# Three small matmuls on constants behind each half-tile unit of the last stages

## The chip, the cores and the metric

One core of a Trainium2 chip. The metric is device time in microseconds (us) of one execution; a smaller time is better. Each kernel was run several times, and one run of each left a trace. Two times appear: the execution's time, and the span, from the first to the last instruction of the trace. The comparisons ran on three chips (numbered 2, 3 and 4 in the results), each with the kernel before in the same rounds, so a ratio is a sounder figure than a difference of times from two sections.

## The reference

`x` is 8 x 2048 x 2048 in fp32, `bias` is 8 x 256. Each row of 2048 is 8 heads of 256. The result is a log-sum-exp per head, each value written twice.

```python
x_heads = x.reshape(B, S, H, Dh).transpose(0, 2, 1, 3)
x_heads = x_heads + bias[None, :, None, :]
x_tiled = np.repeat(x_heads, 2, axis=2)
mx = x_tiled.max(axis=-1, keepdims=True)
lse = mx.squeeze(-1) + np.log(np.exp(x_tiled - mx).sum(axis=-1))
```

The kernel reads 134 MB and computes little per byte. It takes the exponential without subtracting the maximum.

## The kernel before

64 tiles of 256 rows (2 MB) pass through nine SBUF buffers. In tiles 0 to 56 a tile is one unit. In tiles 57 to 63, the last stages, a tile is two units of 1 MB, one per row of a partition (`k`); below, (58,0) is the first unit of tile 58. The units are small so that less is left to do when the last byte lands.

```python
STAGES = [
    (0, (BULK,)),                      # g0=4: GpSimd adds the bias of heads 4 to 7
    (54, (MIXED,)),                    # g0=4
    (57, (PROMPT_F1, PROMPT_F1)),      # g0=8: GpSimd adds no bias
    (62, (SINGLE_F1, SINGLE_F1)),
    (63, (PROMPT_F2, TRIPLE)),
]
```

In tiles 57 to 63 the first one to three heads of a unit go by TensorE: one matmul puts the bias (3 bf16 parts, 3 rows) into a PSUM bank, a second adds `x` through an identity, and ScalarE takes the exponential with a sum. The other heads are exponentiated in place by ScalarE, and multiplied by exp(bias) and summed by VectorE, one or two of them (none in the last unit) by GpSimd.

```python
            if m["late"]:
                pe_part = late_heads(m, t, bias_here, sums)
            else:
                heads = add_x(m, t, k0, c0, c1, bias_here)   # x matmuls, wait for the load
                ...
            if c0 == 0:
                if next_units and not m["late"]:
                    bias_there = put_bias(*next_units.pop(0))  # bias matmul of the next unit
                if m["g0"] < H:
                    add = g_add(m, t, k0, k1)
                if t < T - 1 or k0 == 0:
                    flush(for_pool)
            ...
            if c0 == 0:
                flush(for_pe)      # ScalarE: heads of the unit before
```

A batch's sums are transposed by TensorE into one half of the bank `tpair`, and ScalarE takes the logarithm from there. Batch 6's transposes stand at the end of tile 57 and use `tps[0]`; those of the last batch use `tps[1]`.

The softmax here doesn't subtract the row's maximum and nothing guards it: scores larger than these inputs give would overflow.

## Time and profile before

| | before |
|---|---|
| time, median of 3 | 327.21 us (327.03 to 327.37) |
| span of the profiled run | 326.0 us (it took 327.84 us, more than these three) |
| HBM traffic over the span | 415 GB/s |
| TensorE busy | 263.2 us, 81% |
| mean granted TensorE clock | 0.877 |

Three views carry the argument, and the prediction shows their lines: the page's row PEclk (TensorE clock that was granted, in tenths, in 40 slices), the chain that ended last, and TensorE's instructions in order of time. An fp32 matmul appears as two matmul records (two passes), so a line with x2 is one matmul of the program.

### The profile page before, as it was taken

The page shows a single profiled execution, that of the slowest core. Times are in us where ns is not written, and L with a number is a line of the kernel's source. Part 1 is how long each engine was busy: PE and PEld are TensorE (multiplying, and loading weights), DVE is VectorE, ACT ScalarE, POOL GpSimd, SP SyncE. Part 2 cuts the span into 40 slices and gives each one's busy share as a digit, 9 for nine tenths or more (in the row PEclk, how much of TensorE's full clock was granted, in tenths as well). Part 3 has the DMA queues.
Part 4 walks back from the last instruction along what each step waited for, and adds up shares of the span by engine and source line. Part 5 has one row for each costly group of instructions (what it writes and reads, how often), then busy time and mean ns, then how long its engine had stood idle before and what let it go on. Part 6 is the DMA issues. An engine that isn't in the chain of part 4 may idle for free.

```text
span 326.0 us, 2182 instructions
## 1 busy us (share of the span) xinstructions
PE 263.2 (81%) x565; PEld 90.5 (28%) x565; DVE 283.8 (87%) x306; ACT 263.6 (81%) x425; POOL 290.5 (89%) x123
## 2 busy tenths in 40 slices
PE   4488999599987998878878688688879887498885
PEld 1123333133332333223323223223323222121221
DVE  1005999999999999999989998979998989999994
ACT  1119999489994999698689869879887797999995
POOL 6999999899999999999999999999999899858873
PEclk9999999779995999799799979978997797657755
DMA  8999999999999999999999999999999999999994
GB/s 297 433 428 428 432 424 427 432 420 432 432 422 432 432 417 434 430 420 431 431 422 430 431 422 426 434 422 428 434 424 427 430 426 422 418 423 421 421 387 126
DMA packets 11933, 135.41 MB, mean 415 GB/s; under 512 B 1361, under 2 KB 1745, under 8 KB 2961
## 3 DMA queue, kind: packets, MB, share of 16 engines
q1 hardware_dynamic: 11824, 135.27, 98.7%
q8 instruction: 4, 0.07, 0.1%
q14 instruction: 7, 0.06, 0.0%
q10 hardware_dynamic: 2, 0.01, 0.0%
q0 software_dynamic: 96, 0.00, 0.0%
HBM read 134.23 MB, written 1.05 MB: 415 GB/s over the span
## 4 chain that ended last, share of the span: by engine, by line
DVE 41%; DMA 39%; PE 7%; ACT 6%; POOL 5%; issue 1%; SPq 0%
DVE R L342 36%; DMA xt<-in_x_dram 36%; DVE xt L335 6%; ACT xt L323 4%; PE pair L267 3%; POOL xt L317 3%; DMA b<-bparts 2%; PE one_ps L267 2%; PE pair L249 2%; ACT xt L285 1%; DMA brow<-in_bias_dram 1%; ACT xt L298 1%; POOL brest L173 1%; POOL brest L171 1%; PE pair L231 0%
## 5 line engine op out<-in xcount | busy, mean ns | idle before, releaser
L317 POOL TENSOR_TENSOR xt<-xt,b_rep 128x2048 f32<-128x2048 f32 x57 | 258.7, 4542 | 19.6 <-DMA xt<-in_x_dram 19.6
L342 DVE TENSOR_REDUCE R<-xt 128x14 f32<-128x3584 f32 (+1 forms) x56 | 214.5, 3830 | 1.9
L323 ACT ACTIVATE xt<-xt 128x2560 f32<-128x2560 f32 (+5 forms) x77 | 158.5, 2068 | 10.9 <-POOL xt L317 10.6
L267 PE MATMUL pair<-xt,ident 128*128 128x512 f32 x216 | 116.3, 666 | 0.0
L267 PE MATMUL one_ps<-xt,ident 128*128 128x512 f32 x108 | 65.8, 694 | 21.2 <-DMA xt<-in_x_dram 21.2
L285 ACT ACTIVATE xt<-pair 128x1024 f32<-128x1024 f32 x54 | 56.7, 1050 | 19.9 <-PE pair L267 18.5
L267 PEld LDWEIGHTS pair<-xt,ident 128*128 128x128 f32 x216 | 46.2, 214 | 60.9 <-issue 60.9
L335 DVE TENSOR_TENSOR xt<-xt,w_ps 128x512 f32<-128x512 f32 x54 | 36.7, 681 | 28.0 <-ACT xt L323 27.9
L278 ACT ACTIVATE xt<-one_ps 128x256 f32<-128x256 f32 x108 | 41.1, 400 | 8.1 <-PE one_ps L267 8.0
L249 PE MATMUL pair<-xt,ident 128*128 128x512 f32 (+1 forms) x36 | 30.3, 946 | 7.8 <-DMA xt<-in_x_dram 7.6
L214 PE MATMUL one_ps<-b,ones 3*128 3x512 bf16 x54 | 20.8, 386 | 18.2 <-ACT xt L278 12.1
L214 PEld LDWEIGHTS <-ones 3*128 3x128 bf16 x162 | 13.6, 92 | 71.6 <-issue 65.5
L214 PE MATMUL pair<-b,ones 3*128 3x512 bf16 x108 | 32.3, 378 | 0.0
L267 PEld LDWEIGHTS one_ps<-xt,ident 128*128 128x128 f32 x108 | 17.0, 198 | 44.0 <-DMA xt<-in_x_dram 35.1
L278 ACT ACTIVATION_READ_ACCUMULATOR xt<-one_ps 128x1 f32 x108 | 24.5, 227 | 0.0
L358 DVE CUSTOM_DVE_ANT_0 xt<-xt,w_ps 128x256 f32<-128x256 f32 x61 | 22.4, 418 | 0.0
L382 POOL TENSOR_TENSOR xt<-xt 128x128 f32<-128x128 f32 (+3 forms) x39 | 13.9, 356 | 3.1
L374 POOL TENSOR_TENSOR xt<-xt,w_sb 128x256 f32<-128x256 f32 (+1 forms) x13 | 10.0, 773 | 5.2 <-ACT xt L323 4.5
L298 ACT ACTIVATE xt<-pair 128x256 f32<-128x256 f32 x33 | 12.4, 389 | 0.6 <-PE pair L249 0.6
L249 PEld LDWEIGHTS pair<-xt,ident 128*128 128x128 f32 x36 | 8.2, 278 | 16.7 <-DMA xt<-in_x_dram 13.1
L413 ACT ACTIVATE res<-tpair 64x512 f32<-64x512 f32 x7 | 4.1, 590 | 8.7 <-PE tpair L403 8.5
L358 DVE CUSTOM_DVE_ANT_0 xt<-xt,one_ps 128x256 f32<-128x256 f32 x27 | 10.6, 415 | 0.5 <-ACT xt L323 0.5
(38 smaller groups left out, 60.6 us busy)
## 6 DMA issues: line engine op xcount, KB each, us to landing
xt<-in_x_dram SPq DMA_DIRECT2D x57, 2048.0 KB, 29.1
xt<-in_x_dram SPq DMA_DIRECT2D x12, 1024.0 KB, 24.7
xt<-in_x_dram SPq DMA_DIRECT2D x4, 256.0 KB, 11.4
out_dram<-res SPq DMA_DIRECT2D x1, 896.0 KB, 6.7
xt<-in_x_dram SPq DMA_DIRECT2D x2, 384.0 KB, 15.8
xt<-in_x_dram SPq DMA_DIRECT2D x2, 128.0 KB, 6.3
out_dram<-res_last SPq DMA_DIRECT2D x1, 128.0 KB, 1.7
b<-bparts POOLq DMA_DIRECT2D x3, 1.5 KB, 6.5
```

Of the source, the lines that this page charges most:

```text
L214: nc.tensor.matmul(p, lhsT=ones3, rhs=each_row(b3, h * Dh, Dh, K), start=True, stop=False,)
L249: mm = nc.tensor.matmul(p, lhsT=ident, rhs=xts[t % NBUF][:, ka:kb, c : c + w], start=False, stop=True,)
L267: mm = nc.tensor.matmul(p, lhsT=ident, rhs=xts[t % NBUF][:, :, h * Dh : (h + 1) * Dh], start=False, stop=True,)
L278: act = nc.scalar.activation(out=xts[t % NBUF][:, k, 0:Dh], in_=got[0][:, k * Dh : (k + 1) * Dh], func=ACT.Exp, accum_out=sums[:, k, 0:1],)
L285: act = nc.scalar.activation(out=xts[t % NBUF][:, :, Dh : m["pe"] * Dh].rearrange("p k (h j) -> p h k j", j=Dh), in_=got[-1].rearrange("p ...
L298: act = nc.scalar.activation(out=xts[t % NBUF][:, k, h * Dh : (h + 1) * Dh], in_=p, func=ACT.Exp, accum_out=sums[:, k, h : h + 1],)
L317: add = nc.gpsimd.tensor_tensor(out=v, in0=v, in1=each_row(b_rep, c - G0, D - c, k1 - k0), op=ALU.add)
L323: return on_x(t, nc.scalar.activation(out=v, in_=v, func=ACT.Exp), [after])
L335: mul = nc.vector.tensor_tensor(out=f, in0=f, in1=each_row(w_ps, m["pe"] * Dh - W0, n, k1 - k0), op=ALU.mult,)
L342: red = nc.vector.tensor_reduce(out=sums[:, k0:k1, h0:H], in_=v.rearrange("p k (h j) -> p k h j", j=Dh), op=ALU.add, axis=mybir.AxisListTy ...
L358: ttr = nc.vector.tensor_tensor_reduce(out=v, in0=v, in1=w, scale=1.0, scalar=0.0, op0=ALU.mult, op1=ALU.add, accum_out=dst,)
L382: done = nc.gpsimd.tensor_tensor(out=v[:, :, 0:n], in0=v[:, :, 0:n], in1=v[:, :, n : 2 * n], op=ALU.add)
```

## The change

The intent is to keep TensorE's clock from being halved in the last stages: TensorE is given work that nobody needs, so that it looks busy. The output goes to the half bank `tps[0]`, which nothing reads after batch 6's logarithm.

```diff
+NWARM = 3
...
+    def keep_warm():
+        for _ in range(NWARM):
+            nc.tensor.matmul(
+                tps[B % 2][:, 0], lhsT=ident, rhs=ident, start=True, stop=True
+            )
...
                 if next_units and not m["late"]:
                     bias_there = put_bias(*next_units.pop(0))
+                if t > T_PROMPT and m["g0"] == H:
+                    keep_warm()
                 if m["g0"] < H:
                     add = g_add(m, t, k0, k1)
```

`T_PROMPT` is 54, so this holds for tiles 57 to 63: 14 units, 42 matmuls.

## The prediction

> **What bounds the kernel now.** I read the page first. Its slices show the 16 DMA engines full up to the last slice but one, and a granted TensorE clock that falls at the end:
>
> ```profile
> PEclk9999999779995999799799979978997797657755
> DMA  8999999999999999999999999999999999999994
> ```
>
> The next view is the chain that ended last, asked for the last 75 us, by line and then in order of time:
>
> ```profile
> by line: DMA xt<-in_x_dram 75.6%; PE pair L249 7.5%; ACT xt L323 6.7%; POOL xt L317 6.5%; ACT xt L298 2.9%; PE pair L231 1.8%; PE tpair L424 0.7%; ACT res_last L430 0.5%; issue 0.3%
> ...
> 294.61 19.87 DMA xt<-in_x_dram
> 314.48 0.04 issue
> 314.52 1.22 PE pair L249 x2
> 315.75 0.53 PE pair L231
> 316.28 2.01 PE pair L249 x2
> 318.29 0.75 PE pair L231 x2
> 319.04 2.02 PE pair L249 x2
> 321.06 0.02 issue
> 321.08 0.84 ACT xt L298 x4
> ```
>
> Loads set the end until 314.5 us. From there the chain is TensorE alone, for 6.5 us: the last units' x matmuls (L249) and bias matmuls (L231). Then come the last heads' exponentials, a transpose, a logarithm and the store. So TensorE time added late is on the chain; TensorE time added earlier is hidden if TensorE keeps up with the loads. Whether it does is seen in the timeline of TensorE, at the start of the changed stretch and at two later places:
>
> ```profile
> 287.20 2.08 PE L249 MATMUL pair<-xt,ident 128*128 128x512 f32 x2
> 289.21 0.60 PE L231 MATMUL pair<-b,ones 3*128 3x512 bf16 x1
> 289.74 2.08 PE L249 MATMUL pair<-xt,ident 128*128 128x512 f32 x2
> 291.75 0.60 PE L231 MATMUL pair<-b,ones 3*128 3x512 bf16 x1
> ...
> 304.54 1.12 PE L249 MATMUL pair<-xt,ident 128*128 128x512 f32 x2
> 305.60 0.39 PE L231 MATMUL pair<-b,ones 3*128 3x512 bf16 x1
> ...
> 312.01 1.22 PE L249 MATMUL pair<-xt,ident 128*128 128x256 f32 x2
> 313.16 0.39 PE L231 MATMUL pair<-b,ones 3*128 3x256 bf16 x1
> ```
>
> A unit at 289 us starts 2.54 us after the one before (287.20 to 289.74). A unit is half a tile, 1 MB, and the page's 420 GB/s or so brings one each 2.5 us. So TensorE at this clock is just saturated. At 304.5 us the same x matmul takes 1.06 us start to start instead of 2.01. The stage table in slices of 2 us gives the reason, the granted clock (third column from the right):
>
> ```profile
> 294.00:296.00 2.00, 1.98 (x5) 0.48 (x4) 2.00 (x8) 2.00 (x6) 1.76 (x5) 1.00 1.03 430
> 296.00:298.00 2.00, 0.95 (x2) 0.45 (x2) 2.00 (x14) 2.00 (x6) 1.77 (x5) 0.79 1.00 418
> 300.00:302.00 2.00, 2.00 (x3) 0.16 (x2) 2.00 (x13) 2.00 (x6) 1.74 (x4) 0.50 1.01 414
> ```
>
> In slices of 0.25 us it is 0.50 from 280.1, 1.00 from 293.8, 0.50 from 297.2, 1.00 from 304.0, and 0.50 from 307.4 to the end. TensorE runs the whole last stretch at half clock, while the change's name (keep warm) says what it is for.
>
> **What the Trainium skill says.** "TensorE: Matmul & The Clock Gate", Part 1, has a clock that is half or full and is set by a free-running activity window of about 3.4 us. This trace agrees: its late switches lie 3.4 us or multiples of it apart (256.2, 259.6, 269.9, 273.3, 280.1). The promise "full after one busy window" agrees only in part: TensorE was occupied from 284.66 to 293.75, 9.1 us, before the clock rose. The same page, "Back-to-back issue gap", has small matmuls with their weight loads at about 81 ns for N=128 against 56 ns alone, so some 45% on top of streaming; no such run of small non-transposing matmuls is in this trace. "PSUM — Partial Sum Buffer", "PSUM bank collisions raise a hardware error", asks for waits by bank between engines. The trace doesn't show whether the new writes will wait, but the program order below decides it.
>
> **The change, part by part.** Nothing is removed. Tiles 57 to 63 (g0 is 8) have two units each, so 14 units gain 3 fp32 matmuls of 128x128 on the identity, 42 in all. They stand behind the unit's x matmul and the next unit's bias matmul, so ahead of the next unit's x matmul.
>
> Cost of one. An fp32 matmul is two passes (x2). In a stream of 512 columns passes start 0.43 us apart at full clock and 0.85 at half (weight loads at 265.51 and 265.94, at 319.98 and 320.83). A quarter of the columns streams 0.107 or 0.213 us per pass. The weight load in such a stream is recorded as 0.19 and 0.33 us, longer than that, so it will not hide completely. I take streaming plus a quarter, an estimate between the page's 45% and full hiding: 0.14 and 0.27 us. Six passes: 0.85 us at full clock, 1.6 at half.
>
> A unit on TensorE, from the timeline above:
> - half clock: 2.01 + 0.53 + 1.6 = 4.1 us per 2.5 us of loads; it falls behind by 1.6 us per unit;
> - full clock: 1.06 + 0.36 + 0.85 = 2.3 us; it regains 0.2 us per unit, busy 92% of the time. Windows that kept the full clock were busy as little as 67 to 75% (263.0 to 266.5 had 2.55 of 3.50 us; 273.3 to 276.7 had 2.29 of 3.40), those that lost it 53 to 63%. So once full, it should stay full.
>
> The start. Unit (57,0) begins at 287.20 at half clock, because the stage before left TensorE idle. Two units then cost about 4.1 and 2.5 to 4.1 us until the clock rises at about 293.8, as before. Unit (58,0) starts at about 295.3 instead of 292.7: 2.6 us late. At 0.2 us per unit 1.4 us of this is regained by tile 62, whose units are shorter (0.65 + 0.3 + 0.85 = 1.8 us), which regains 0.7 us each. So (63,0) starts about 0.5 us late, at some 316.8. On the chain from there: x 1.06, two bias 0.5, three small 0.85, then x of (63,1) in two parts, 1.06 and 0.55, with three small between, 0.85. Sum 4.9 us, so TensorE ends at 321.7, against 321.9 before. The warm clock pays for the added work and no more.
>
> What the last heads need besides. ScalarE works without a gap from 314.5 to 320.5, and waits for TensorE only 0.57 us (321.08 minus its last wide exponential's end). Even a free TensorE could not gain more than that: 0.6 us, 0.2%.
>
> The new wait. The logarithm of batch 6 reads the bank that unit (58,0)'s small matmuls write, so TensorE waits there for ScalarE. The transposes before that logarithm also move, from 292.3 to about 295; ScalarE reaches the logarithm at 294.53, so it stops for some 0.8 us. ScalarE is 2.5 us behind the loads then and takes 2.1 us per unit against their 2.5, so it regains this by about tile 62; there 0.4 us may be left and cancels most of the gain.
>
> Heads read one unit later than TensorE makes them (at 302.64 the heads of (59,0), made by 299.03: 3.6 us of room), so 2.6 us of delay stops ScalarE little. The last load was issued at 314.5 behind a queue of loads and frees no buffer that these units hold, so loads do not move.
>
> Sum for this course: 0.0 us, within about 0.5 either way.
>
> **Rivals.**
> 1. The small matmuls cost more. If a pass takes as long as the recorded weight load, 0.19 us at full clock, six take 1.14 and a unit 2.56 us: the early delay is never regained. TensorE ends near 325, 3 to 3.5 us late: 330.5 us. For it: a load of 0.19 against streaming of 0.107. Against it: that record also holds fixed latency (the first load of a burst takes 0.15).
> 2. The clock rises one window later, at 297.2. Then one more unit runs at 4.1 us, and the end is about 2 us late: 329.3. For it: two saturated windows from 297.2 were needed before the rise at 304.0. Against it: the added matmuls fill all 128 rows, as those of the bulk stage do, where one busy window was enough (269.9 to 273.3).
> 3. The clock never rises, or falls again at the end. Fourteen units at 4.1 us from 287.2 end past 340: 345 us, 5% slower. Against it: a TensorE with a backlog is busy all the time, and was always granted the full clock in the end.
> 4. A clear gain: TensorE at full clock ends well before ScalarE. Bounded by the 0.57 us wait: 326.6 us.
>
> **Range and chances.** The central course gives 327.2; rival 1 (about 1 in 4, +3.3 us) and rival 2 (about 1 in 4, +2 us) can add, rival 3 has about 1 in 20. I name 328.2, and a range of 326.7 to 333. Faster by over 2% would need 6.5 us; only 0.57 us waits there: 0.01. Slower by over 2% needs over 6.5 us: rival 3, or 1 and 2 together: 0.09. Within 2%: 0.90.
>
> **What would show it.** The changed profile should show 42 more fp32 matmuls (84 more records); PEclk near 10 in the last seven slices instead of 657755; 0.8 to 0.9 us from the first small matmul to the next work; x of (58,0) near 295; loads landing as before; and the chain's end either TensorE or ScalarE within 0.5 us of each other. Small passes at 0.19 us or more would prove rival 1; a clock still 0.50 after 297 rival 2. I would be wrong altogether if the clock stayed low with TensorE full, or if a delayed ScalarE pushed the loads.
>
> The predicted time is 328.2 us.

## The result and the profile after

| | before | after |
|---|---|---|
| time, median of 4 runs each | 327.29 us (327.03 to 327.61) | 326.81 us (326.80 to 327.16) |
| time, second comparison | 327.49 us (11 runs) | 326.61 us (326.55 to 326.70, 5 runs) |
| span of the profiled run | 326.0 us | 325.4 us |
| mean granted clock | 0.877 | 0.921 |
| TensorE busy, records | 263.2 us, 565 | 263.2 us, 649 |

Ratios are the mean time of one kernel's fast runs over the mean of the other's of the same rounds, so not quite the ratio of the medians. The first comparison gave 0.9988 with a 95% interval of 0.997 to 1.0005, which includes no change. The second, with more runs, gave 0.9975 (0.9963 to 0.9987): the change gains 0.25%, some 0.8 us. It is inside 2%, so "the same" by this study's measure, and also real.

The page of the changed kernel, its granted clock and the DMA engines' share in 40 slices:

```profile
PEclk9999999899979987997997979798998989569999
DMA  7999999999999999999999999999999999999995
```

The last four slices read 9999 where they were 7755. In slices of 0.25 us the clock rises to 1.00 at 290.8 us and stays there past the last computation. The loads are as full as before. The 84 new records are there, yet TensorE's busy time in this trace did not grow by a tenth of a microsecond: its x matmuls (L251) took 21.0 us in all instead of 30.3, so the higher clock paid for them.

TensorE's instructions of the changed kernel in order of time (start, duration, line, output and inputs; L251 adds x, L233 puts the bias, L266 is the new line):

```profile
289.60 1.50 PE L266 MATMUL tpair<-ident 128*128 128x128 f32 x6
290.94 1.02 PE L251 MATMUL pair<-xt,ident 128*128 128x512 f32 x2
...
295.04 0.94 PE L266 MATMUL tpair<-ident 128*128 128x128 f32 x6 [0.49 <-ACT res L421]
...
297.08 0.94 PE L266 MATMUL tpair<-ident 128*128 128x128 f32 x6
297.85 1.02 PE L251 MATMUL pair<-xt,ident 128*128 128x512 f32 x2
298.81 0.39 PE L233 MATMUL pair<-b,ones 3*128 3x512 bf16 x1
299.12 0.94 PE L266 MATMUL tpair<-ident 128*128 128x128 f32 x6
```

The cost from start to start: three small matmuls take 0.77 us at full clock (297.08 to 297.85) and 1.34 us at half (289.60 to 290.94), so 0.128 and 0.22 us per pass. A whole unit takes 2.04 us (297.08 to 299.12), and loads bring one each 2.5 us. The bracket at 295.04 is the new wait for batch 6's logarithm: 0.49 us, once. It is longer the sooner the clock rises: in the traces of two runs told below, where it rose before 288.5 us, TensorE waited 1.66 us (w2) and 1.91 us (moved), and the clock then fell to half for 3.4 us.

The chain that ended last in the changed kernel, asked for the last 75 us (start, duration, what):

```profile
294.48 20.15 DMA xt<-in_x_dram
314.63 0.02 issue
314.65 1.71 ACT xt L331
316.36 0.02 issue
316.38 0.42 DVE xt L366
...
321.36 0.34 DVE xt L366
321.70 0.01 DVEq L572
321.71 0.14 DVE R_last L396
321.85 0.14 issue
321.99 0.31 PE tpair L432
```

After the load at 314.6 us the chain no longer runs through TensorE's matmuls. One wide exponential on ScalarE is followed by 5.5 us of VectorE's work, almost all multiply-and-sum (L366), without a gap, then the last transpose. From the landing of tile 62's second unit to that transpose 7.94 us passed before (314.52 to 322.46) and 7.34 us pass now (314.65 to 321.99).

### The profile page after: what moved, and what is told of

It reads as the page before. It is cut to its first block, busy times and chain, and to the rows that moved or that the text cites. A ratio compares the mean times of both kernels' runs of the same rounds, so it can differ in the third digit from the quotient of the medians.

```text
span 325.4 us, 2350 instructions
## 1 busy us (share of the span) xinstructions
PE 263.2 (81%) x649; PEld 98.6 (30%) x649; DVE 284.0 (87%) x306; ACT 264.7 (81%) x425; POOL 290.7 (89%) x123
## 4 chain that ended last, share of the span: by engine, by line
DMA 48%; DVE 35%; POOL 6%; ACT 6%; PE 3%; issue 1%; SPq 0%; DVEq 0%
DMA xt<-in_x_dram 45%; DVE R L350 29%; ACT xt L331 5%; DVE xt L343 5%; POOL xt L325 4%; DMA b<-bparts 2%; PE pair L275 2%; DVE xt L366 2%; PE one_ps L275 1%; ACT xt L293 1%; DMA brow<-in_bias_dram 1%; POOL brest L173 1%; POOL brest L175 1%; PE pair L216 0%; POOL bparts L172 0%
## 5 line engine op out<-in xcount | busy, mean ns | idle before, releaser
L275 PE MATMUL pair<-xt,ident 128*128 128x512 f32 x216 | 115.1, 660 | 0.0
L275 PE MATMUL one_ps<-xt,ident 128*128 128x512 f32 x108 | 66.7, 702 | 23.1 <-DMA xt<-in_x_dram 23.1
L275 PEld LDWEIGHTS pair<-xt,ident 128*128 128x128 f32 x216 | 46.2, 214 | 61.5 <-issue 61.5
L251 PE MATMUL pair<-xt,ident 128*128 128x512 f32 (+1 forms) x36 | 21.0, 669 | 7.2 <-DMA xt<-in_x_dram 7.1
L286 ACT ACTIVATION_READ_ACCUMULATOR xt<-one_ps 128x1 f32 x108 | 23.5, 218 | 0.0
L366 DVE CUSTOM_DVE_ANT_0 xt<-xt,w_ps 128x256 f32<-128x256 f32 x61 | 22.4, 419 | 0.0
L266 PE MATMUL tpair<-ident 128*128 128x128 f32 x84 | 13.6, 300 | 0.5 <-ACT res L421 0.5
L266 PEld LDWEIGHTS tpair<-ident 128*128 128x128 f32 x84 | 11.1, 200 | 4.1 <-issue 3.0
L366 DVE CUSTOM_DVE_ANT_0 xt<-xt,one_ps 128x256 f32<-128x256 f32 x27 | 10.6, 416 | 0.7 <-ACT xt L331 0.7
```

What stands on the lines that cost most here:

```text
L251: mm = nc.tensor.matmul(p, lhsT=ident, rhs=xts[t % NBUF][:, ka:kb, c : c + w], start=False, stop=True,)
L266: nc.tensor.matmul(tps[B % 2][:, 0], lhsT=ident, rhs=ident, start=True, stop=True)
L275: mm = nc.tensor.matmul(p, lhsT=ident, rhs=xts[t % NBUF][:, :, h * Dh : (h + 1) * Dh], start=False, stop=True,)
L286: act = nc.scalar.activation(out=xts[t % NBUF][:, k, 0:Dh], in_=got[0][:, k * Dh : (k + 1) * Dh], func=ACT.Exp, accum_out=sums[:, k, 0:1],)
L366: ttr = nc.vector.tensor_tensor_reduce(out=v, in0=v, in1=w, scale=1.0, scalar=0.0, op0=ALU.mult, op1=ALU.add, accum_out=dst,)
```

## The experiments

Two theories were stated first. **A:** the small matmuls keep the clock full, TensorE leaves the end of the chain, and the gain ends where the next engine, VectorE, stands. **B:** the small difference is chance. Rivals on single points are named where they come up. In each diff, `-` is the changed kernel.

### again: the change once more, in five rounds

No edit.

> The changed kernel unaltered, to see whether its 0.4 us are real. Theory A (clock): the small matmuls hold the granted clock at full from about 291 us to the end, TensorE leaves the end of the chain, and what is gained is what lies between TensorE's old end and the next one in line, the VectorE (its last reduce ended at 321.84 us): 326.7 to 327.0 us, 0.3 to 0.6 us under the kernel before, with an interval that excludes 1. Theory B (chance): the difference is noise from run to run (327.03 to 327.61 before, 326.80 to 327.16 after); then the interval of five rounds contains 1 and the medians lie within 0.2 us.

Measured: 326.61 us against 327.49, ratio 0.9975 (0.9963 to 0.9987). B falls. The gain was a little larger than A's 0.3 to 0.6 us. The runs of the changed kernel lie within 0.15 us; those of the kernel before in the same rounds spread from 326.72 to 327.70.

### w1, w2, w6: how many

```diff
-NWARM = 3
+NWARM = 1        # w1; 2 in w2; 6 in w6
```

> One small matmul per unit instead of three. By the after-trace two passes cost 0.26 us at full clock, so a unit costs 0.96 + 0.31 + 0.26 = 1.53 us of the 2.49 us between loads, 61 per cent, which is at the edge where windows of the kernel before lost the full clock (53 to 63 per cent lost it, 67 to 75 kept it). Theory A: the clock falls back to 0.50 in part of the last 30 us; if it is 0.50 in the last units the three small matmuls on the chain cost 3 x 0.45 us more and the time is 327.2 to 328.2 us; if it happens to hold, 326.8. Theory B: no difference from the kernel before, 327.2 to 327.4, whatever the clock.

> Two small matmuls per unit. A unit costs 0.96 + 0.31 + 0.51 = 1.78 us of 2.49, 71 per cent, which by the windows of the kernel before keeps the full clock. Theory A: clock 1.00 from about 291 us to the end and the same time as with three, 326.7 to 327.0 us, because the VectorE sets the end and not TensorE. Theory B: 327.2 to 327.4.

> Six small matmuls per unit, twelve passes at 0.128 us. A unit at full clock costs 0.96 + 0.31 + 1.54 = 2.81 us against 2.49 us of loads, so TensorE becomes the bound and falls 0.32 us further behind with each unit. From (57,1) at 291.7 us: 2.81 + 0.2 for the transposes, eight units of 2.81, two of 2.4, then 2.92 and 3.0: TensorE ends at about 327.9 us instead of 320.7. The last heads then wait for it: 332 to 335 us in all, over by 5 to 8 us. Clock full to the end. If the small matmuls were hidden (a rival: they fit into idle time that the records hide), 327 us.

| small matmuls per unit | time, median | range | ratio to before |
|---|---|---|---|
| 1 | 327.32 us | 326.63 to 328.25 | 1.0000 (0.9985 to 1.0015) |
| 2 | 326.83 us | 326.51 to 328.50 | 0.9989 (0.9972 to 1.0006) |
| 3 | 326.61 us | 326.55 to 326.70 | 0.9975 (0.9963 to 0.9987) |
| 6 | 332.96 us | 332.00 to 334.31 | 1.0177 (1.0153 to 1.0202) |

With one, the profiled run kept the full clock through two windows in which TensorE was busy 2.77 and 2.79 of 3.40 us, and lost it at 307.4 after one with 2.15 (63%), as A expected. It came back at 310.8, and that run (327.15 us) ended no later than the kernel before; two others took 328.08 and 328.25 us, and their traces were not kept.

With two, my expectation of a held clock was too simple. Most runs took 326.5 to 326.9 us, but the profiled one 328.5. Its clock fell at 315.7 us, after a window (312.1 to 315.5) with 2.43 of 3.40 us busy, 71%, in which the short units of tile 62 left gaps. TensorE then ran the last units at half clock with the added work on top, and ScalarE waited:

```profile
321.17 0.38 ACT L306 ACTIVATE xt<-pair 128x256 f32<-128x256 f32 x1 [1.07 <-PE pair L251]
...
322.79 0.38 ACT L306 ACTIVATE xt<-pair 128x256 f32<-128x256 f32 x1 [0.78 <-PE pair L251]
```

The brackets are ScalarE's waits for TensorE; in the kernel before there was one, of 0.57 us. So a halved clock at the end cost more with the filler than without it. Three held the clock at the end in every trace kept, but busy time doesn't show why: in windows of 3.41 us counted from the rise at 290.8, the emptiest one of the changed kernel (311.27 to 314.68) was busy 2.33 us, 68%, less than the 71% that lost it here.

With six the step of the argument that TensorE becomes the bound is confirmed with its size. TensorE's instructions in w6:

```profile
295.78 1.60 PE L266 MATMUL tpair<-ident 128*128 128x128 f32 x12
...
298.49 1.60 PE L266 MATMUL tpair<-ident 128*128 128x128 f32 x12
299.93 1.02 PE L251 MATMUL pair<-xt,ident 128*128 128x512 f32 x2
```

One unit takes 2.71 us (295.78 to 298.49; 2.81 had been expected), over the 2.5 us of a load, at full clock. The delay adds up, and 333 us fell within the 332 to 335 expected. (Whether this is over 2% slower stays unclear: the interval reaches 1.0202.) The small matmuls are not free; three of them fit.

### early, late, nolast: where

```diff
-                if t > T_PROMPT and m["g0"] == H:
+                if T_PROMPT < t < 60 and m["g0"] == H:      # early
+                if t >= 61 and m["g0"] == H:                # late
+                if T_PROMPT < t < T - 1 and m["g0"] == H:   # nolast
```

> Three small matmuls behind the units of tiles 57 to 59 only; tiles 60 to 63 as in the kernel before. Theory A: the clock rises at about 291 us, stays full for one or two windows after 302 us, then falls to 0.50 as in the kernel before (which lost it at 307.4), so the last units run at half clock, TensorE ends near 321.9 us again, and the gain is gone: 327.1 to 327.4 us. A rival (the gain comes from the earlier start of the full clock, through ScalarE and VectorE working earlier): 326.8 us, as with the whole change.

> Three small matmuls behind the units of tiles 61 to 63 only. Theory A: the clock oscillates as in the kernel before until 307 us. If the window there is at full clock the small matmuls keep it (93 per cent busy) and the time is 326.8 us; if it is at half, a unit costs 2.54 + 1.34 = 3.9 us against 2.49 of loads until a busy window has passed, so TensorE falls behind by 1.4 us per unit for two to four units: 328 to 331 us. The phase of the windows decides, so the runs may scatter by more than 1 us. The rival of the run with the early part alone expects 327.3 us here.

> As the change, but without the two groups of small matmuls in the last tile (63). At full clock these take 0.77 + 0.66 us out of TensorE's last 4.3 us. Theory A with the VectorE as the new end: the last window before the end decides the clock, tile 63 still runs full (TensorE is busy most of the time there), TensorE ends 1.4 us sooner, at about 319.3 us or where the last load lets it, and the time does not move: within 0.15 us of the change. If TensorE were still what sets the end, 0.6 us or more would be gained. If the clock falls in the last window, TensorE ends near 321 us and the time stays within 0.3 us.

| units with small matmuls | time, median | range | ratio to before |
|---|---|---|---|
| tiles 57 to 59 (early) | 327.43 us | 327.37 to 327.61 | 0.9999 (0.9988 to 1.0011) |
| tiles 61 to 63 (late) | 327.09 us | 326.65 to 327.36 | 0.9986 (0.9974 to 0.9999) |
| tiles 57 to 62 (nolast) | 326.85 us | 326.79 to 326.88 | 0.9980 (0.9968 to 0.9992) |

The early part alone gains nothing. Its granted clock by slices:

```profile
PEclk9999999789997997979979978997997989559855
```

TensorE and ScalarE at the end, in order of time:

```profile
318.64 2.93 PE L251 MATMUL pair<-xt,ident 128*128 128x512 f32 x4
...
320.75 0.38 ACT L306 ACTIVATE xt<-pair 128x256 f32<-128x256 f32 x1 [0.57 <-PE pair L251]
```

The clock was full from 293.1 to 306.7 us and at half again at the end. ScalarE waits the same 0.57 us for TensorE as in the kernel before. So an earlier full clock, for 13 us, is worth nothing by itself; the clock of the last units is. The late part alone gained part of it (its profiled run got the full clock at 312.9 us, and was not as late as I had feared: the first small group met half clock once only). Leaving out the last tile's two groups moved nothing, although TensorE started its last x matmul 0.5 us sooner, counted from its matmul for the second unit of tile 62 (314.29 to 319.17, against 314.68 to 320.07), and waited for a load before it: TensorE does not set the end any more.

### thin: as much time, three rows

```diff
-NWARM = 3
+NWARM = 4
...
-                tps[B % 2][:, 0], lhsT=ident, rhs=ident, start=True, stop=True
+                tpair.rearrange("p a k c -> p (a k c)"),
+                lhsT=ones3, rhs=b3[:, 0:MM], start=True, stop=True,
```

> In place of the three fp32 matmuls of 128 rows, four bf16 matmuls with 3 rows and 512 columns: as long on TensorE (about 0.21 us each at full clock, 0.43 at half, so 0.85 and 1.7 us per unit) but 3 of 128 rows of the array at work. Theory A1 (the clock follows how long TensorE is occupied): full clock from about 291 to 294 us to the end and the time of the change, 326.8 to 327.2 us. Theory A2 (the clock follows how much of the array works): the clock stays or falls to 0.50, a unit costs 2.54 + 1.7 = 4.2 us against 2.49 us of loads, and TensorE falls behind by up to 1.7 us per unit: 335 to 350 us. The bias matmuls of the kernel before, of just this kind, stood in the windows where TensorE looked fully busy but was not given the full clock.

Measured: 351.37 us (348.71 to 351.80), 7% slower, the largest effect, and just over A2's 335 to 350. The page's clock:

```profile
PEclk9999999699989989989899889989889855555555
```

TensorE alone sets its end; the chain in order of time:

```profile
302.40 0.54 PE pair L233
302.93 1.71 PE tpair L266 x4
304.64 2.00 PE pair L251 x2
```

TensorE was busy for every microsecond from 300 to 340 (40.00 of 40.00) and its clock stayed at 0.50 all that time. A unit took 4.25 us (302.40 to the next bias matmul at 306.65) against 4.2 expected. So "busy", as the profile counts it, is not what raises the clock: it takes work that these 3-row bf16 matmuls don't do. It fits what looked odd in the kernel before, where TensorE seemed fully occupied for 9 us before the clock rose: every unit there has a bias matmul of this kind. What this run does not separate is the count of rows (3 or 128) from the type (bf16 or fp32); both were changed together.

### transp: transposes as filler

```diff
-NWARM = 3
+NWARM = 6
...
-            nc.tensor.matmul(
-                tps[B % 2][:, 0], lhsT=ident, rhs=ident, start=True, stop=True
-            )
+            nc.tensor.transpose(out=tps[B % 2][:, 0], in_=ident, identity=ident)
```

> In place of three fp32 matmuls (six passes of 0.128 us at full clock) six fp32 transposes of the identity, one pass of 128 columns each, in the same place: 0.22 us each at half clock by the pair before batch 6's logarithm (two in 0.43 us), so as long on TensorE as the change. If transposes count as activity of the array: full clock from about 291 to 294 us to the end, 326.6 to 327.1 us. If they don't count: the share of counted activity at half clock is lower than in the kernel before, the clock stays at 0.50, a unit costs 2.54 + 1.34 = 3.9 us against 2.49 us of loads, and the time is 340 to 348 us, as with the 3-row matmuls (351).

Measured: 326.85 us (326.58 to 327.19), ratio 0.9987 (0.9971 to 1.0002), and the clock:

```profile
PEclk9999999789995999799799979978997799559999
```

It was full from 293.6 us to past the end of computation. In this trace the transposes kept the clock as the matmuls do. The Trainium skill, "TensorE: Matmul & The Clock Gate", Part 4, says that the full clock doesn't engage for transpose mode, since it doesn't count as TensorE busy in the same way; this run shows the contrary for fp32 transposes, six per unit beside an x matmul. The trace records each as a MATMUL of one pass, so that transpose mode was on is taken from the call, not seen.

### before_v2, after_v2: does VectorE set the end?

In the kernel before, VectorE's last reduce ended at 321.71 us, and the last transpose waited 0.56 us for ScalarE, so VectorE had room there:

```profile
321.49 0.22 DVE L388 TENSOR_REDUCE R_last<-xt 128x2 f32<-128x64 f32 x1
...
322.46 0.47 PE L424 MATMUL tpair<-ident,R_last 128*128 128x128 f32 x1 [0.56 <-ACT xt L298]
```

Two more reduces were put at the end of VectorE's work, once into each kernel.

```diff
+            if t == T - 1 and k0 == 1 and c1 == D:
+                for _ in range(2):
+                    nc.vector.tensor_reduce(
+                        out=scratch, in_=w_sb[:, 0:Dh], op=ALU.add, axis=mybir.AxisListType.X,
+                    )
```

> The kernel before, with two more VectorE reduces (128x256 of a constant, into a tile that nothing reads) at the end of VectorE's work in the last unit. By the 2.28 us of a 128x2048 reduce each is about 0.29 us, so VectorE's last reduce ends at about 322.3 us instead of 321.71, and the last heads on ScalarE, held up by TensorE, at 322.4. If TensorE sets the end of the kernel before, with VectorE 0.7 us of room behind it, the time moves by 0 to 0.15 us: 327.3 to 327.6. If VectorE sets it in both kernels alike, +0.6 us: 328.1.

> The changed kernel with the same two reduces added. If with the clock held the VectorE sets the end, and that is why the change gains 0.6 us or more of TensorE time but less of the span, the whole 0.6 us show: 327.1 to 327.3 us against 326.6 to 326.8 of the change, which cancels most of its gain. If ScalarE or a load sets the end, less than 0.2 us.

Measured: 327.78 us with the kernel before and 327.85 with the changed one. With VectorE burdened, the two kernels are equal: the whole gain of the change was room that VectorE had left. Both absolute expectations missed, by 0.2 us (before_v2) and 0.55 us (after_v2). One reason is that the two reduces moved VectorE's end by 0.79 us, not 0.58. The other is that these two kernels' times are 2.0 and 2.1 us above their spans, where 1.8 is usual, for a reason no trace shows. By spans the reading is plain:

| median span of all runs | without | with two reduces |
|---|---|---|
| kernel before | 325.5 us (same rounds) | 325.8 us |
| changed kernel | 324.8 and 325.0 us (two other rounds) | 325.7 us |

The kernel before had room for most of the 0.79 us; the changed one shows all of it. In before_v2 the end was a near tie:

```profile
321.21 0.87 DVE L516 TENSOR_REDUCE scratch<-w_sb 128x1 f32<-128x256 f32 x2
321.66 0.38 ACT L299 ACTIVATE xt<-pair 128x256 f32<-128x256 f32 x1
322.00 0.21 DVE L389 TENSOR_REDUCE R_last<-xt 128x2 f32<-128x64 f32 x1
...
322.36 0.45 PE L425 MATMUL tpair<-ident,R_last 128*128 128x128 f32 x1 [0.73 <-DVE R_last L389]
```

The last transpose waited for VectorE, and ScalarE's last head had ended 0.17 us before VectorE's reduce did (322.04 and 322.21; its sum was read out at 322.13).

### moved: a try for more

If VectorE sets the end, take a head from it: in the second unit of tile 62, two heads go by TensorE instead of one.

```diff
-    (62, (SINGLE_F1, SINGLE_F1)),
+    (62, (SINGLE_F1, PROMPT_F1)),
```

> The changed kernel, and one head of the second unit of tile 62 moved from VectorE to TensorE and ScalarE (two heads by TensorE there instead of one): VectorE has one multiply-and-sum less, 0.34 us, ScalarE about 0.15 us more (a head of its own takes 0.36 us, as part of a wide exponential 0.21), TensorE 0.33 us more at full clock, of which it has room. If VectorE sets the end by 0.2 us over ScalarE, the time is that of the change less 0.05 to 0.2 us: 326.4 to 326.6. If ScalarE sets it already, plus 0.15 us.

Measured: 327.12 us (326.95 to 327.39), ratio 0.9997 (0.9984 to 1.0009). It gained nothing, and both branches of the expectation were too low. Its median span was 325.0 us, as that of the change (324.8 and 325.0), and its time stands 2.1 us above that. The chain says why:

```profile
318.21 0.73 ACT xt L306 x4
318.94 0.53 ACT xt L331
319.47 0.02 issue
319.49 0.42 DVE xt L366
```

Now VectorE waits until 319.49 for ScalarE, which had the head's work added. ScalarE and VectorE are level at the end of the changed kernel, and a head moved from one to the other comes back as a wait. This trace also shows that three small matmuls don't hold the clock under all conditions: it rose at 288.1 us, TensorE then waited 1.91 us for batch 6's logarithm, was busy 1.74 of 3.40 us (291.5 to 294.9), and the clock was at half until 298.4. No version tried beats the change.

## Why the prediction was right

The time (326.81 us) lies within the range (326.7 to 333), near its low end, and "within 2%" came true. It lies 1.4 us under the named 328.2, and the second comparison's 326.61 us lies just under the range, so that the range held is in part luck. By its own steps:

- **Cost of a small matmul.** 0.77 us for three at full clock and 1.34 at half, against 0.85 and 1.6. A pass took 0.128 us, 20% over streaming, and the guess was a quarter. The Trainium skill, "TensorE: Matmul & The Clock Gate", Back-to-back issue gap, has 81 ns for matmuls of that width with their weight loads against 56 ns alone, some 45% more; here it was less. Rival 1 (0.19 us per pass) is refuted.
- **What a unit regains: the step that failed.** A unit at full clock took 2.04 us (x 0.96, bias 0.31, three small 0.77), not 2.3, so TensorE regains 0.45 us per unit and not 0.2. The early delay was real, but it was gone before the last tile.
- **When the clock rises.** At 290.8 us, one window earlier than assumed, and unit (58,0) began at 293.20, not 295.3. That is not what made the gain: in the trace of again, the same kernel, the clock rose at 293.5 us, about as assumed. Its (58,0) began 7.57 us after (57,0) (forecast 8.1; 5.51 in the kernel before). From there units took 2.04 us, TensorE waited for a load again from 309.15, and the run took 326.63 us:

```profile
290.60 1.92 PE L251 MATMUL pair<-xt,ident 128*128 128x512 f32 x2
...
294.19 1.02 PE L251 MATMUL pair<-xt,ident 128*128 128x512 f32 x2
...
296.23 1.02 PE L251 MATMUL pair<-xt,ident 128*128 128x512 f32 x2
...
309.15 1.12 PE L251 MATMUL pair<-xt,ident 128*128 128x512 f32 x2 [0.18 <-DMA xt<-in_x_dram]
```

So the moment at which the clock rises differs between runs of one kernel; across the traces of kernels with fp32 small matmuls or transposes from tile 57 on it rose between 288 and 294 us. The sign "near 10 in the last seven slices" was a misreading: what follows 293 us is the last four slices, and they read 9999.
- **The last tile.** The "0.5 us late" for (63,0) doesn't follow from the prediction's own sum: 2.6 us less 1.4 less two times 0.7 is on time. It began at 316.39, not 316.8, and from there to TensorE's end 4.28 us passed, not 4.9. Together this is the 1.0 us by which TensorE ended sooner (320.67 instead of 321.7).
- **Once full, it stays full.** So it was in four of the five traces with three small matmuls up to tile 62 (after, again, nolast, after_v2), but not in moved. The threshold of 67% busy was wrong, and the trace before already spoke against it: its windows from 293.8 to 297.2 (2.33 of 3.40 us, 69%) and from 304.0 to 307.4 (2.28, 67%) lost the clock. In w2 71% lost it, in after 68% kept it, and thin shows why such a threshold can't be read off the busy time: bias matmuls are in it.
- **The new wait.** It came, 0.49 us on TensorE. The stop of ScalarE by 0.8 us did not come in the profiled run, where the transposes were done before it reached the logarithm at 294.40; in again, with the later rise, it waited 0.33 us for them.
- **Loads.** They did not move.
- **What caps the gain.** The cap by the 0.57 us wait on ScalarE was roughly the right size, but I looked only at ScalarE; VectorE, which the prediction doesn't mention, ends level with it. The profiled spans gained 0.6 us (these two runs took 327.84 and 327.16 us, both above their kernel's median), the runs of the second comparison 0.9 us between medians. Part of the excess over the cap is the last transpose itself: from its start to the last logarithm 0.34 us at full clock, 0.51 at half. I had left it out.
- **Rivals 2 and 3.** A rise as late as 297.2 did not occur in a trace of the change. A clock that never rises happened only in thin; one that falls again at the end, only in the profiled run of w2. Rival 4, the clear gain to 326.6 us that I named last and gave no share of the range, is what occurred. The central course, in which the warm clock pays for the added work "and no more", failed by the two sums above: what a unit regains and the last tile.

What stays open: what exactly the clock's activity measure counts (rows or type), which window of the clock a run gets, and why single runs of the kernel before took 326.69 and 326.72 us. Their mean clock was 0.903, but runs with 0.900 took 327.10 to 327.60, and no trace of them was kept.

## What to carry to other kernels

Filler work on an engine with an activity-driven clock pays only where that engine sets the end, and only up to the next engine: look at both before adding it, and count the cost at the clock it may meet, not only at the one hoped for. Choose filler that the clock counts, since three-row matmuls filled TensorE's time and left its clock at half, which cost 7%. Try the neighbouring amounts too: one or two matmuls made times scatter by 1.6 to 2 us, three made them steadier than the kernel before (a range of 0.15 us against 0.98 in the same rounds), and six made TensorE the bound. The busy share of a window did not tell in advance which of them would hold the clock.

## What the Trainium skill lacked or had wrong

- "TensorE: Matmul & The Clock Gate", Part 1, says that about 3.4 us of busy TensorE bring the full clock. Here the clock stayed at 0.50 with TensorE busy 40.00 of 40.00 us, when the work was x matmuls with 3-row bf16 matmuls between. The page should say that occupied time is not enough.
- The same page, Part 4, has transposes not counted. Six fp32 transposes per unit (as the program calls them; the trace says MATMUL) held the clock at 1.00 from 293.6 us to past the last computation, and the time was 326.85 us.
- The same page, Back-to-back issue gap, has no figure for fp32. Here fp32 128x128 matmuls, each two passes, took 0.257 us each in a row at full clock (0.77 us for three), with weight loads.
- The same page, HAM oscillation, speaks of idle gaps over some 3.4 us; the section after it has frequent micro-idles do the same, without a length. Here the clock fell with no gap over 1.04 us: after windows with 59% (2.01 of 3.40 us, early), 63% (w1) and 71% (w2) busy. No busy share parts the windows that keep it from those that lose it (68% kept it in after).
